# One pool of equal pages, and an encoder's first mixer interleaved in another order with its neighbours

## The chip, the core and the metric

The kernel runs on one NeuronCore of a Trainium2 chip, as one program. Five engines have instruction streams of their own: TensorE (PE in the profile; PEld is its weight load), VectorE (DVE), ScalarE (ACT), GpSimd (POOL) and SyncE (SP), of which SP and POOL mostly issue DMAs. An engine executes its stream in the order in which it was written; semaphores connect the streams. The metric is the device time of one execution in microseconds (us).

## The reference

A residual stream x of 1024 tokens by 1024 channels, fp32, goes through two layers. Each normalises x, shifts and scales it by a vector computed from the condition c (`ada_w`), applies a mixer, adds the gated result to x, and does the same with a SwiGLU feed-forward. Layer 0's mixer is the one that matters here:

```python
def attention_rwkv_mixer(h, cos, sin, w_in, w_out, ...):
    p = h @ w_in
    q, k, v = ...                      # 8 query heads, 2 key/value heads of 64
    q = apply_rope(rms_norm(q, q_norm), cos, sin)
    k = apply_rope(rms_norm(k, k_norm), cos, sin)
    y_attn = blocked_gqa(q, k, v)      # softmax(q k^T / 8) v, 512 channels
    y_rwkv = rwkv7_bidirectional(p[..., ATTN_IN:], ...)   # 512 channels
    return concat([y_attn, y_rwkv]) @ w_out
```

`rwkv7_bidirectional` runs a recurrence with a 64 by 64 state per head forward and backward over the tokens, adds both, normalises each head's 64 channels (`ln_g`, `ln_b`), adds a bonus and multiplies by a gate. Layer 1's mixer is a Hyena: a projection to three streams, short convolutions, and two long convolutions, whose filters come from a small network of the position and depend on no activation, then an output projection.

## The kernel before, in words

**Products.** Activations stand transposed, channels on the partitions, in tiles of 128 channels by 1024 tokens. Every large operand is split into a high and a low part in a shortened format: `split` lets ScalarE round the high part (L256) and VectorE subtract it (L257). A product is then three: high by high, high by low, low by high (`mm3`, L296), over two halves of 512 tokens. The feed-forward has its own form with seven products of blocks (L600 to L602).

**Pages.** SBUF is cut into equal pages of 128 partitions by 4 KB, handed out first in, first out: `page` takes the one longest free, `free` appends. There are two stacks, one for fp32 and one for the split operands; `repage` re-cuts the space between them between stages, and `fence`, `zone` and `low` keep certain pages from being handed out. An instruction that writes a page handed out anew waits for those that last used it; a DMA's wait stands on the engine that issues it, ahead of all that engine's later issues.

**Order.** Each part is a Python generator that emits a few instructions and yields. `weave` takes the generator that is furthest behind in proportion to its weight; `some(g, n)` takes n steps from g. So the order on every engine is fixed when the program is built.

**The first layer.** `norm_h` makes the normalised activations. The input projection (`stream`) runs over tiles of 128 output channels, with weights loaded on SP (L274), first RWKV tiles (their mixing steps with the neighbouring tokens are L1036, L1045 to L1047) with six attention tiles inserted, of which k and q are normalised and turned (L533, L541, L853). Beside it run `ada(1)` and the first steps of the first RWKV unit (`rwkv_x`, L1187, L1332). A unit is one direction of one pair of heads, eight in all. Then a loop weaves, per iteration i, `rwkv_s` (the scan of unit i-2; L1457 is a step's product, L1458 its state update, L1472 and L1475 its outputs) with a later part of unit i-1, the start of unit i, and n steps of `other`, which is attention (scores L924 and L925, softmax L928 to L932, transposes L947, values) followed by the sixteen Hyena filters (L1740, L1754, L1653, stored by POOL at L1764). After its second scan a pair of heads goes through `rwkv_post`: sums over each head (L1497), L1498, a square (L1501), sums (L533), the root and its inverse (L498, L501, L502), which are spread again (L541), then L1510, L1512, L1513. The result goes to DRAM (`sp_yr`), as do attention's (`sp_ya`).

**After the loop.** The attention half of the output projection (`project`, `matvec_add`, all tokens) and then the other half (`matvec_halves`, one token half after the other) load their operands, split them and add the gated product to x (L787), which the second half does as the feed-forward's normalisation asks for it.

**The Hyena.** Its split weights are loaded from DRAM in pieces (`hwi...` of the input projection, `hwo...` of the output projection) on POOL; L1630 is another operation of POOL's stream.

## Time and profile before

| | us |
|---|---|
| three runs | 3453.62, 3456.78, 3461.62; median 3456.78 |
| the profiled execution | 3456.75 |
| its span (first to last instruction) | 3454.8 |
| TensorE busy in the span | 3248.2 (94%) |
| VectorE busy | 2358.4 (68%) |
| ScalarE busy | 1252.9 (36%) |
| mean granted TensorE clock | 0.964 |

The last loop iteration of the mixer (the scan of the eighth unit) lies from 1238 to 1353 us, the projection behind it until about 1465, the feed-forward until 1900, the Hyena's mixer until 2750. In a row of a timeline stand the start, the duration, engine and line, the operation with its output and inputs, how often it comes in the group, and in brackets the idle time before it and what ended it. A row of DMA issues gives the time of the issue, not of the transfer.

### The profile page before, as it was taken

The numbers are of one execution on the slowest core, as the hardware profiler recorded it, in microseconds if no ns is written. First come the engines' busy times: TensorE is split into PE (matmuls) and PEld (weight loads), VectorE is DVE, ScalarE is ACT, GpSimd is POOL, SyncE is SP. The second block draws the span as 40 slices with busy tenths as digits, with TensorE's granted clock in tenths as the row PEclk, the third lists the DMA queues.
The fourth block names the chain that finished last, engine by engine and source line by source line (L and its number), as shares of the span: only waits on it lengthen the run. The fifth ranks groups of instructions, "written<-read, shape, count | busy, mean of one in ns | idle before, by whom it ended". The sixth has DMA issues, their size and how long they took to land.

```text
span 3454.8 us, 52847 instructions
## 1 busy us (share of the span) xinstructions
PE 3248.2 (94%) x20739; PEld 2635.1 (76%) x20739; DVE 2358.4 (68%) x4281; ACT 1252.9 (36%) x2296; POOL 245.0 (7%) x509
## 2 busy tenths in 40 slices
PE   8899889999999997999999999989977799999998
PEld 5687767777677896888888887777866688888887
DVE  5466465656667777597877667588997776667545
ACT  4632265555554442343233333221220243333211
POOL 2000000000011221000000220000000000000000
PEclk9999999999999998999999999999998899999999
DMA  7654522233332326244455993324335522224411
GB/s 260 226 174 147 162 62 72 59 87 80 82 104 71 94 81 201 80 128 146 134 162 191 356 359 129 119 80 140 128 127 206 173 78 93 74 73 137 142 50 49
DMA packets 332536, 459.29 MB, mean 133 GB/s; under 512 B 102968, under 2 KB 234897, under 8 KB 332288
## 3 DMA queue, kind: packets, MB, share of 16 engines
q1 hardware_dynamic: 292576, 322.04, 30.4%
q0 software_dynamic: 39536, 133.81, 11.3%
q8 instruction: 163, 2.67, 0.3%
q14 instruction: 85, 0.70, 0.1%
q10 hardware_dynamic: 176, 0.07, 0.0%
HBM read 311.66 MB, written 141.56 MB: 131 GB/s over the span
## 4 chain that ended last, share of the span: by engine, by line
PE 62%; DVE 8%; DMA 4%; issue 3%; ACT 2%; POOL 0%; DVEq 0%; SPq 0%; ACTq 0%; POOLq 0%
PE bk L296 21%; PE bk L601 8%; PE bk L602 8%; PE bk L600 8%; PE bk L1754 3%; DVE p L1653 2%; PE bk L1740 2%; PE bk L1775 2%; DMA p<-in_hy_w_in_dram 1%; PE bk L1928 1%; PE bk L947 1%; PE bk L1268 1%; PE bk L1332 1%; PE bk L1785 1%; PE bk L964 1%
## 5 line engine op out<-in xcount | busy, mean ns | idle before, releaser
L296 PE MATMUL bk<-p,p 128*128 128x512 f32 x5136 | 1242.8, 401 | 72.9 <-ACT p L256 33.2
L296 PEld LDWEIGHTS bk<-p,p 128*128 128x128 f32 x5136 | 980.7, 193 | 298.0 <-ACT p L256 36.0
L256 ACT ACTIVATE p<-p 128x512 fp32r<-128x512 f32 (+3 forms) x534 | 398.4, 761 | 950.8 <-PE bk L601 287.8
L257 DVE TENSOR_TENSOR p<-p,p 128x512 fp32r<-128x512 f32 (+3 forms) x534 | 445.7, 850 | 255.2 <-ACT p L256 215.6
L600 PE MATMUL bk<-p,p 128*128 128x512 f32 x1248 | 486.3, 391 | 2.7 <-ACT p L256 1.4
L601 PE MATMUL bk<-p,p 128*128 128x512 f32 x1248 | 486.0, 390 | 2.5 <-DVE p L257 2.5
L602 PE MATMUL bk<-p,p 128*128 128x512 f32 x1248 | 484.6, 390 | 0.0
L600 PEld LDWEIGHTS bk<-p,p 128*128 128x128 f32 x1248 | 234.5, 188 | 52.4 <-ACT p L256 4.3
L601 PEld LDWEIGHTS bk<-p,p 128*128 128x128 f32 x1248 | 235.0, 188 | 51.7 <-DVE p L257 3.3
L602 PEld LDWEIGHTS bk<-p,p 128*128 128x128 f32 x1248 | 234.6, 188 | 48.8
L787 DVE SCALAR_TENSOR_TENSOR p<-bk,mod,p 128x512 f32<-128x512 f32 x192 | 134.8, 744 | 90.0 <-PE bk L296 86.8
L1653 DVE TENSOR_TENSOR p<-p 128x128 f32<-128x128 f32 (+2 forms) x544 | 174.1, 384 | 0.2 <-ACT p L1309 0.2
L429 DVE SCALAR_TENSOR_TENSOR p<-p,cond,p 128x512 f32<-128x512 f32 x140 | 104.6, 748 | 54.3 <-DMA p<-in_ada_w_dram 52.1
L1754 PE MATMUL bk<-p,p 128*128 128x128 f32 x1024 | 135.0, 287 | 0.0
L1754 PEld LDWEIGHTS bk<-p,p 128*128 128x128 f32 x1024 | 125.9, 199 | 5.6 <-issue 2.0
L928 DVE TENSOR_REDUCE mx<-bk 128x1 f32<-128x512 f32 x128 | 87.1, 686 | 56.5 <-PE bk L925 55.4
L1742 ACT ACTIVATE p<-delta,k_tneg 128x128 f32<-128x128 f32 x256 | 86.9, 393 | 70.4 <-PE bk L1754 10.2
L1036 ACT COPY p<-bk 128x512 f32<-128x512 f32 (+1 forms) x80 | 43.9, 588 | 182.9 <-DVE p L1802 63.6
L948 ACT COPY p<-bk 128x512 f32<-128x512 f32 x128 | 74.1, 587 | 95.5 <-PE bk L947 94.2
L932 ACT ACTIVATE p<-bk,mx 128x512 f32<-128x512 f32 x128 | 86.9, 686 | 34.9 <-DVE mx L929 34.2
L947 PE MATMUL bk<-k_ident,p 128*128 128x128 f32 x512 | 85.0, 293 | 15.3 <-ACT p L932 14.8
L478 ACT ACTIVATE p<-p 128x512 f32<-128x512 f32 x80 | 49.9, 633 | 126.2 <-DVE p L814 117.6
(407 smaller groups left out, 4392.4 us busy)
## 6 DMA issues: line engine op xcount, KB each, us to landing
p<-in_ffn_w_dram SPq DMA_DIRECT2D x120, 512.0 KB, 4.8
p<-in_ada_w_dram SPq DMA_DIRECT2D x96, 512.0 KB, 4.4
sp_f<-p POOLq DMA_DIRECT2D x36, 512.0 KB, 5.5
p<-sp_f POOLq DMA_DIRECT2D x36, 512.0 KB, 5.7
hs<-p POOLq DMA_DIRECT2D x64, 256.0 KB, 3.2
p<-hs SPq DMA_DIRECT2D x32, 512.0 KB, 4.2
p<-sp_r SPq DMA_DIRECT2D x24, 512.0 KB, 4.8
p<-sp_x SPq DMA_DIRECT2D x24, 512.0 KB, 4.4
```

The source lines that it names most:

```text
L256: self.nc.scalar.activation(out=hi, in_=src, func=AF.Copy)
L257: self.nc.vector.tensor_tensor(out=lo, in0=src, in1=hi.bitcast(F32), op=ALU.subtract)
L296: nc.tensor.matmul(ps[n], a, b[:, HALVES[n]], start=s, stop=e)
L429: nc.vector.scalar_tensor_tensor(out=acc, in0=wt[:, i], scalar=self.cond[:, k : k + 1], in1=acc, op0=ALU.mult, op1=ALU.add)
L600: nc.tensor.matmul(ps, op[:, 0, k], mh, start=start and k == 0, stop=False)
L601: nc.tensor.matmul(ps, op[:, 0, k], ml, start=False, stop=False)
L602: nc.tensor.matmul(ps, op[:, 1, k], mh, start=False, stop=stop and k == 3)
L787: nc.vector.scalar_tensor_tensor(out=xs, in0=ps[n], scalar=self.modc(layer, part, m), in1=xs, op0=ALU.mult, op1=ALU.add)
L928: nc.vector.tensor_reduce(out=m[:, n : n + 1], in_=ps[n], axis=AX.X, op=ALU.max)
L947: nc.tensor.transpose(pt[:, j], pr[:, k * P : (k + 1) * P], self.ident)
L1653: tt = lambda o, a, b, op: nc.vector.tensor_tensor(out=o, in0=a, in1=b, op=op)
L1754: nc.tensor.matmul(ps[:, j, ri], F[2 * d + t2 // 4][:, t2 % 4, 128 * ri : 128 * ri + 128], tp[:, j, d], start=d == 0, stop=d == 1)
```

## The change

There is one pool of 46 pages, each of which may hold either kind of operand; `repage`, `fence`, `zone` and `low` are gone. Attention's six tiles in the projection move: k and the first two q from places 13, 15, 17 to 10, 11, 12, and v, last, from 21 to 20. `early` emits, beside the projection, the first RWKV unit's start and then the first step of attention (the keys, the first queries and the first scores). Attention loads its values only when it needs them. In the loop the steps of `other` change so that the filters end before the last iteration, and there `other` becomes `mix_out`: the attention half of the output projection, a fourth of a product at a time (`fine`), then the weights and the first three operands of the other half. The last pair of heads is split where it is made (`pair`), without the trip through DRAM. `project` gives x in SBUF (`kept`) to the second half.

```diff
-        self.stacks = {F32: [], F32R: []}
-        self.pages = {F32: deque(), F32R: deque()}
+        self.pages = deque()
...
+    def paging(self, ctx, n):
+        self.sb = ctx.enter_context(self.tc.tile_pool(name="sb", bufs=1))
+        self.pages.extend(range(n))
+        self.n = 0
...
-        t = next(z[dt] for z in self.zone if z[dt]).popleft()
+        i = self.pages.popleft()
+        self.n += 1
+        t = self.sb.tile([P, PAGE], dt, tag=f"pg{i}", name=f"p{self.n}")
+        self.page_of[t.tensor.name] = i
...
-                dt, t, _ = self.page_of[a.tensor.name]
-                assert all(t is not q for q in self.pages[dt])
-                self.put(t)
+                self.pages.append(self.page_of.pop(a.tensor.name))
...
+    def matvec_add(self, xT, w, ys, layer, part, g=0, keep=None, fine=False):
...
-                self.mm3(ps, [(wt[0][:, k, o : o + P], wt[1][:, k, o : o + P]) for k in range(nk)], ys)
+                wk = [(wt[0][:, k, o : o + P], wt[1][:, k, o : o + P]) for k in range(nk)]
+                for k in range(nk):
+                    self.mm3(ps, wk[k : k + 1], ys[k : k + 1], k == 0, k == nk - 1)
+                    if fine and k < nk - 1:
+                        yield
...
+            if "v" not in st:
+                st["v"] = self.page((P, 8, P))
+                nc.gpsimd.dma_start(out=st["v"].rearrange("p a b -> p (a b)"), in_=self.vd)
+            v = st["v"]
...
-                    self.fence(F32R, first=4)
...
-            out[hp] = self.rwkv_post(ys.pop(hp), hp, G)
+            out[hp] = self.rwkv_post(ys.pop(hp), hp, G, hp == 3)
...
+        if pair:
+            return self.split(y)
...
-        tiles = self.rwkv_tiles()
-        for i, t in zip((13, 15, 17, 19, 20, 21), self.attn_tiles()):
-            tiles.insert(i, t)
-        weave((250, self.stream(w, h, tiles)), (60, ada(1)), (30, first()))
-        for a in h:
-            self.free(a)
-        self.repage(42, 4)
-        self.set_banks(4, 4)
+        other = None
+
+        def early():
+
+            yield from first()
+            while not {"k", 0} <= set(self.qd):
+                yield "wait"
+            yield from some(other, 1)
...
+        tiles = self.rwkv_tiles()
+        for i, t in zip((10, 11, 12, 17, 19, 20), self.attn_tiles()):
+            tiles.insert(i, t)
+        weave((250, self.stream(w, h, tiles)), (60, ada(1)), (32, early()))
+        for a in h:
+            self.free(a)
+        self.set_banks(4, 4)
         for i in range(1, len(units) + 2):
             if i == len(units):
                 self.free(self.scanm)
-            n = (0, 48, 48, 48, 48, 50, 48, 46, 50, 48)[i]
+            n = (0, 48, 50, 52, 54, 54, 54, 62, 84, 36)[i]
+            if i > len(units):
+                run(other)
+                other = tail([out[x] for x in range(4)], outr)
...
-        for _ in other:
-            pass
+        run(other)
         self.set_banks(8)
-        return [out[i] for i in range(4)] + [outr[i] for i in range(4)]
...
+    K.paging(ctx, 46)
...
-    def project(xT, ys, w, layer, g=0):
+    def project(xT, ys, w, layer, g=0, **how):
 
         y = [K.split(K.unspill(d)) for d in ys]
         yield
-        yield from K.matvec_add(xT, w, y, layer, 2, g)
+        yield from K.matvec_add(xT, w, y, layer, 2, g, **how)
...
+    def mix_out(ya, yr):
+
+        w = ins["mix_w_out"][0]
+        yield from project(xd, ya, w[:512], 0, 1, keep=kept, fine=True)
+        y = []
+        steps.append(K.matvec_halves(kept, w[512:], y, 0, 2))
+        for i in range(3):
+            y.append(K.split(K.unspill(yr[i])))
+        while 3 not in yr:
+            yield
+        y.append(yr[3])
...
-    w = ins["mix_w_out"][0]
-    ys = K.mixer(ins["mix_w_in"][0], h, ada)
-    K.repage(13, 33)
-    xT = [K.unspill(d) for d in xd]
-    run(project(xT, ys[:4], w[:512], 0))
-    xT, steps = K.ffn(xT, halves(xT, ys[4:], w[512:], 0), 0, ada1(), hy_weights(), 20)
+    kept, steps = [], []
+    K.mixer(ins["mix_w_in"][0], h, ada, mix_out)
+    xT, steps = K.ffn(kept, steps[0], 0, ada1(), hy_weights())
```

The line numbers of the changed kernel differ: its L258 is the old L296, L883 and L884 are L924 and L925, L906 is L947, L1294 is L1332, L495 and L503 are L533 and L541, L1419 is L1457, L1434 and L1437 are L1472 and L1475, L1459 is L1497, L236 is L274 and L168 is L206. In the rows p is a page, bk a PSUM bank.

On TensorE, the end of the mixer's loop before, from the last sums of heads on:

```order
L1497 MATMUL bk_66<-p_158,k_blkones 128x512
L1754 MATMUL bk_68<-p_82,p_102 128x128
...
L1754 MATMUL bk_64<-p_3006,p_130 128x128
L1497 MATMUL bk_63<-p_158,k_blkones 128x512
L533 MATMUL bk_70<-k_blk_77,p_3010 128x2 x8
L541 MATMUL bk_65<-k_ident,rc_1277 64x128 x8
L541 MATMUL bk_63<-k_ident,rc_1277 64x128 x8
L296 MATMUL bk_66<-p_234,p_11458 128x512
```

All of the projection's products (L296) stand behind the last L541. And now, from the scan's last output on; p_12287 is the high part of the last pair of heads:

```order
L1459 MATMUL bk_64<-p_11372,k_blkones 128x512
L258 MATMUL bk_67<-p_12230,p_12211 128x512
L258 MATMUL bk_67<-p_12229,p_12212 128x512
...
L258 MATMUL bk_69<-p_12235,p_12218 128x512
L495 MATMUL bk_65<-k_blk_77,p_12254 128x2 x8
L258 MATMUL bk_65<-p_12223,p_12199 128x512
...
L258 MATMUL bk_65<-p_12235,p_12200 128x512
L503 MATMUL bk_66<-k_ident,rc_1151 64x128 x8
L503 MATMUL bk_70<-k_ident,rc_1151 64x128 x8
L258 MATMUL bk_66<-p_12223,p_12205 128x512
...
L258 MATMUL bk_70<-p_12235,p_12206 128x512
L258 MATMUL bk_64<-p_12287,p_12199 128x512
```

The filters' products between the sums have given way to products of the second half's first three operands, and 18 products now follow the last L503 ahead of the first that needs the last pair. Further ahead, the 192 products of the attention half stand between the scan's steps, but for the last five:

```order
L1434 MATMUL bk_66<-p_9435,p_10870 64x64
L1434 MATMUL bk_66<-p_9436,p_10870 64x64
L1437 MATMUL bk_66<-p_11525,p_11896 64x64 x2
L1434 MATMUL bk_66<-p_9435,p_10870 64x64
L1419 MATMUL bk_64<-p_11896,p_11524 64x64 x2
...
L258 MATMUL bk_67<-p_12223,p_12211 128x512
L258 MATMUL bk_67<-p_12224,p_12211 128x512
...
L258 MATMUL bk_69<-p_12229,p_12217 128x512
L1419 MATMUL bk_64<-p_11896,p_11524 64x64 x10
L1437 MATMUL bk_65<-p_11525,p_11896 64x64 x2
```

A step of the scan (two L1419) stood between filters before; the ten L1419 in one row are the last five steps.

On TensorE, attention's first scores before, behind the whole projection:

```order
L296 MATMUL bk_65<-p_554,p_258 128x512
L296 MATMUL bk_65<-p_550,p_482 128x512
L1332 MATMUL bk_70<-p_98,p_138 64x64 x11
L551 MATMUL bk_66<-k_ident,p_118 128x128 x3
L541 MATMUL bk_64<-k_ident,rc_2105 64x128 x8
L541 MATMUL bk_63<-k_ident,rc_2105 64x128 x8
L551 MATMUL bk_66<-k_ident,p_118 128x128
L1332 MATMUL bk_70<-p_98,p_138 64x64 x5
L551 MATMUL bk_64<-k_ident,p_118 128x128 x4
L1332 MATMUL bk_63<-p_98,p_142 64x64 x16
L924 MATMUL bk_64<-p_234,p_242 128x512
```

Here nothing of the projection (L296) is left to stand behind the first L924. And now, where the first scores stand in the last tiles' products and the first transposes (L906) behind the last of them:

```order
L495 MATMUL bk_63<-k_blk_77,p_2775 128x2 x7
L883 MATMUL bk_68<-p_2726,p_2734 128x512
...
L495 MATMUL bk_63<-k_blk_77,p_2775 128x2
L258 MATMUL bk_64<-p_414,p_2676 128x512
...
L884 MATMUL bk_68<-p_2727,p_2734 128x512
L884 MATMUL bk_69<-p_2727,p_2734 128x512
L258 MATMUL bk_65<-p_414,p_2677 128x512
...
L258 MATMUL bk_70<-p_419,p_2782 128x512
L1149 MATMUL bk_65<-p_2432,k_blkones 128x512
L883 MATMUL bk_68<-p_2726,p_2735 128x512
L884 MATMUL bk_68<-p_2727,p_2735 128x512
...
L906 MATMUL bk_69<-k_ident,p_2754 128x128 x4
```

L883 has moved ahead of the last tile's L258, and the first L906 behind them.

On SP, at the start of the kernel, the issues from the last constant of the first group to the first weight of the projection, before:

```order
L114 DMA k_eye_671<-in_k_eye_dram 128x64
L1526 DMA p_146<-in_k_scanm_dram 128x1040
L830 DMA p_150<-in_k_rope_c_dram 128x1024
L831 DMA p_154<-in_k_rope_s_dram 128x1024
L206 DMA sp_x_700<-p_94 128x1024
L206 DMA sp_x_714<-p_98 128x1024
L274 DMA p_158<-in_mix_w_in_dram 128x8x128
L206 DMA sp_x_740<-p_102 128x1024
```

The first weight (L274) stands behind two stores of x. And now, where eight stores of x and more small loads stand ahead of that weight:

```order
L108 DMA k_eye_460<-in_k_eye_dram 128x64
L1582 DMA hy_w<-in_hy_f_w_dram 33x64
L168 DMA sp_x_498<-p_125 128x1024
...
L168 DMA sp_x_847<-p_132 128x1024
L1584 DMA hy_w<-in_hy_f_w_dram 64x64 x2
...
L108 DMA k_tneg<-in_k_tneg_dram 128x16
L1030 DMA p_563<-in_rwkv_w_up_dram 64x2x512 x2
L1491 DMA p_468<-in_k_scanm_dram 128x1040
L791 DMA p_470<-in_k_rope_c_dram 128x1024
L792 DMA p_471<-in_k_rope_s_dram 128x1024
L236 DMA p_474<-in_mix_w_in_dram 128x8x128
```

The first weight (L236) has moved behind all of these, the weights of L1030 (before: L1067) among them.

More of the change, by code (lines that the diff above doesn't have):

```diff
@@ L553, in to_tok, with ffn @@
             self.fbank(pt)
-    def ffn(self, xT, before, layer, up=iter(()), down=iter(()), low=None):
+    def ffn(self, xT, before, layer, up=iter(()), down=iter(())):
         nc = self.nc
@@ L884, in attention @@
         nc = self.nc
-        v = self.page((P, 8, P))
-        nc.gpsimd.dma_start(out=v.rearrange("p a b -> p (a b)"), in_=self.vd)
         st = {}
@@ L996, in attention @@
                 yield from values(*steps[i - 1][:2])
-        self.free(st["k"], v)
+        self.free(st["k"], st["v"])
     def rwkv_spec(self):
@@ L1517, in rwkv_post, with mixer @@
         return d
-    def mixer(self, w, h, ada):
+    def mixer(self, w, h, ada, tail):
         self.rwkv_consts()
```

60 lines of the change are left out of this document (4 added, 56 removed).

## The prediction

> **What bounds the kernel now.** First the page's busy times. TensorE is busy for 94% of the span, VectorE for 68%:
>
> ```profile
> PE 3248.2 (94%) x20739; PEld 2635.1 (76%) x20739; DVE 2358.4 (68%) x4281; ACT 1252.9 (36%) x2296; POOL 245.0 (7%) x509
> ```
>
> The change leaves the products as they are, so the 3248.2 us of TensorE work stay. What can move is the 206.6 us of the span (3454.8 less 3248.2) in which TensorE stands idle, and the slower clock just after such gaps. A table of windows then finds the gaps: the mixer's loop by its iterations (the start, iterations 6 to 9), then the projection behind it.
>
> ```profile
> 427.00:514.00 87.00, 73.88 (x838) 55.54 (x840) 59.47 (x122) 52.56 (x122) 3.09 (x7) 0.90 0.25 64
> 917.00:1027.00 110.00, 100.96 (x1238) 81.14 (x1236) 72.58 (x196) 56.12 (x134) 14.27 (x25) 0.97 0.24 74
> 1027.00:1142.00 115.00, 103.57 (x1166) 89.86 (x1166) 82.64 (x237) 49.76 (x136) 21.24 (x34) 0.93 0.34 81
> 1142.00:1238.00 96.00, 96.00 (x1178) 85.33 (x1178) 64.73 (x198) 44.67 (x124) 22.91 (x35) 0.96 0.32 91
> 1238.00:1353.00 115.00, 90.58 (x733) 82.03 (x729) 94.01 (x278) 42.23 (x105) 27.78 (x42) 0.89 0.52 167
> 1365.00:1465.00 100.00, 100.00 (x459) 83.27 (x458) 51.23 (x78) 31.27 (x51) 0.00 (x0) 1.00 0.22 74
> ```
>
> After the stretch come PE, PEld, DVE, ACT and POOL busy, then the granted clock. Two rows stand out, with clocks of 0.90 and 0.89: the first loses 13.1 us, the last iteration 24.4 us. The last row gives the price of one long product with TensorE full: 100/459 = 0.218 us. The feed-forward stages are full in the same way and have nothing to give.
>
> **Part one, the mixer's end.** The timeline shows the 24.4 us as three gaps in one chain, the normalisation of the last head pair and its trip through DRAM:
>
> ```profile
> 1317.90 0.69 DVE L1498 SCALAR_TENSOR_TENSOR p<-bk,p 128x512 f32<-128x512 f32 x1 [0.36 <-PE bk L1497]
> 1324.38 1.04 ACT L1501 ACTIVATE p<-p 128x1024 f32<-128x1024 f32 x1
> 1325.48 2.57 PE L533 MATMUL bk<-k_blk,p 128*128 128x2 f32 x16 [3.18 <-ACT p L1501]
> 1329.21 1.28 ACT L501 ACT_TABLE_LOAD   x1
> 1334.33 3.68 PE L541 MATMUL bk<-k_ident,rc 128*64 128x128 f32 x32 [6.28 <-DVE rc L502]
> 1338.68 1.40 DVE L1510 SCALAR_TENSOR_TENSOR p<-p,cols,bk 128x512 f32<-128x512 f32 x2
> 1340.11 1.28 DVE L1512 SCALAR_TENSOR_TENSOR p<-p,cols,p 128x1024 f32<-128x1024 f32 x1
> 1343.33 1.22 DVE L1513 TENSOR_TENSOR p<-p,p 128x1024 f32<-128x1024 f32 x1
> 1345.96 0.32 SPq L211 DMA_DIRECT2D p<-sp_ya  x1
> 1351.86 1.06 ACT L256 ACTIVATE p<-p 128x1024 fp32r<-128x1024 f32 x1 [6.22 <-DMA p<-sp_ya]
> 1352.96 12.30 PE L296 MATMUL bk<-p,p 128*128 128x512 f32 x44 [14.96 <-ACT p L256]
> ```
>
> 3.18 + 6.28 + 14.96 = 24.42, the window's whole idle time. The slow clock adds 44 products in 12.30 instead of 9.6 us (2.7) and 32 L541 in 3.68 us against the 1.97 they take at 421.81 (1.7). Together 28.8 us.
>
> The new order puts 192 products of the attention half (192 x 0.218 = 41.9 us) and 54 of the other half (11.8 us) beside the scan, where before the filters stood. What is left bare, step by step: five scan steps without a product between them, each a wait for one L1458 and its handover (0.28 us and about 0.2, an estimate), 5 x 0.45 = 2.2; the handover to the first L1497, 1.1; L1498 and L1501 (1.73) lie under 17 products (3.7), 0; from L533 to L541 the table load 1.28 and three short steps, some 2.5, under 9 products (2.0), 0.5; from L541 the chain 1.40 + 1.28 + 1.22 + 1.06 = 4.96, with handovers 5.8, under 18 products (3.9), 1.9. That is 5.7. I add 2 for the clock after several short gaps (a gap of 1.3 us is followed by slow products in a row of part three), and 3 because VectorE, which runs in order, also has the residual adds and splits of the projection in this stretch.
>
> The moved step also brings its own loads: sp_ya, the weights and eight sp_x on SP's queue, where before they were issued during the filters' tail. The first products stand on TensorE ahead of the scan's next L1457, so if a load is late, the scan is too. The nearest row is the load above, 5.9 us from issue to L256. From 0 (loaded ahead) to 6; I take 4, since one page of it comes free only with the last filters' stores. After: 5.7 + 2 + 3 + 4 = 14.7. **Gain 14** (7 to 21).
>
> **The filters moved.** They no longer stand beside the last scan but in iterations 6, 7 and 8 (some 2, 1 and 2.7 filters more than before, by the order). Iterations 9 and 8 differ by 1.9 filters and 94.01 - 64.73 = 29.3 us of VectorE, so about 15 each. VectorE then has 72.58 + 29 = 102, 82.64 + 15 = 98 and 64.73 + 41 = 105 us. TensorE gets at least the 8.4 us of a filter's L1754, to 117, 112 and 118:
>
> ```profile
> L1754 PE MATMUL bk<-p,p 128*128 128x128 f32 x1024 | 135.0, 287 | 0.0
> ```
>
> 135.0/16 = 8.4. So TensorE stays the bound, by a narrower margin. **Cost 3** (-4 to +8): iterations 6 and 7 had 9.0 and 11.4 us of gaps, which more filter work may fill, or attention and scan may wait longer for the fuller VectorE.
>
> **Part two, the mixer's start.** Attention's first scores wait for the rope's normalisation and then their softmax stalls TensorE:
>
> ```profile
> 421.81 1.97 PE L541 MATMUL bk<-k_ident,rc 128*64 128x128 f32 x32
> 429.93 1.97 PE L1332 MATMUL bk<-p,p 64*64 64x64 f32 x32 [4.82 <-DVE p L853]
> 432.14 2.08 PE L924 MATMUL bk<-p,p 128*128 128x512 f32 x4 [0.24 <-ACT p L894]
> 434.02 1.88 PE L925 MATMUL bk<-p,p 128*128 128x512 f32 x4
> 443.77 1.97 PE L947 MATMUL bk<-k_ident,p 128*128 128x128 f32 x8 [7.88 <-ACT p L932]
> ```
>
> 4.82 + 0.24 + 7.88 = 12.9 idle, and the eight products take 3.96 instead of 8 x 0.218 = 1.7 us: 15.1. Now keys and the first queries are projected earlier and L924 and L925 stand among the last tile's products, with 55 of them (12.0 us) between the first pair of L925 and the first L947. From the end of L925 to L947 it was 7.9 us, so this gap goes. What is late next is the last projected tile, now a value tile of the RWKV half. Its mixing steps are:
>
> ```profile
> 83.54 1.15 ACT L1046 ACTIVATE p<-p,mu 128x1024 f32<-128x1024 f32 x1
> 84.50 1.23 DVE L1045 TENSOR_TENSOR p<-p 128x1024 f32<-128x1024 f32 x1
> 85.83 1.28 DVE L1047 SCALAR_TENSOR_TENSOR p<-p,mu,p 128x1024 f32<-128x1024 f32 x1
> ```
>
> About 3.7 us with copies and handovers 5, under scores, transposes and L1332 of similar length. I leave 4 us idle and 2 for slow clock. **Gain 9** (3 to 14).
>
> **Part three, one pool.** At the start of the kernel the order of SP's issues changes. Before:
>
> ```profile
> 36.37 0.33 SPq L114 DMA_DIRECT2D k_eye<-in_k_eye_dram  x1
> ...
> 41.95 0.95 SPq L274 DMA_DIRECT2D p<-in_mix_w_in_dram  x1
> ...
> 53.92 1.22 PE L296 MATMUL bk<-p,p 128*128 128x512 f32 x2
> ...
> 58.23 1.02 SPq L274 DMA_DIRECT2D p<-in_mix_w_in_dram  x2
> ...
> 69.92 15.74 PE L296 MATMUL bk<-p,p 128*128 128x512 f32 x61 [1.10 <-DVE p L257]
> ...
> 91.42 1.22 PE L1085 MATMUL bk<-p,p 128*128 128x512 f32 x2 [5.76 <-DVE p L1071]
> ```
>
> From k_eye to the second weight there were 18 issues in 21.9 us, 1.2 each. Now the first weight has 20 issues between k_eye and itself, so it is issued at about 36.4 + 24 = 60.4, 18 us later, and its products begin near 68 instead of 53.9 (issue, transfer and split, about 8 us, less than the first one's 12 since the queues are emptier). But then 96 run in one piece, 20.9 us, to 89, where before they were broken up and L1085 came at 91.42, because its weights were issued at 76.95; now those go ahead. **0** (-5 to +9).
>
> Behind the first feed-forward, the hyena's projection waits for loads issued by POOL, which itself stands behind a wait for VectorE:
>
> ```profile
> 2136.18 8.61 PE L296 MATMUL bk<-p,p 128*128 128x512 f32 x24 [1.30 <-DMA p<-hwi1l]
> 2164.16 8.57 PE L296 MATMUL bk<-p,p 128*128 128x512 f32 x25 [4.83 <-DMA p<-hwi8h]
> POOL p L1630 <- DVE p L522: 18.9, 1, 18.9
> ```
>
> Idle 6.1, slow clock 3.4 + 3.1, together 12.6. In the new order the load behind the second gap waits on products some 70 places ahead of its use (15 us), the load behind the first on some 25 (5.5 us, about the length of a load). **Gain 5** (-4 to 12).
>
> One rule of the Trainium skill is weighed here. The first of these rows is slow, 8.61 us for 24 products, after a gap of 1.30 only. The page "TensorE: Matmul & The Clock Gate" (section "HAM oscillation — how this bites in real kernels") has the clock fall only where TensorE idles for more than some 3.4 us at a time. By it the short gaps left at the mixer's end would cost no clock, part one would gain 16, and the sum below would be 2 us lower. The row disagrees with it, so the 2 us stay.
>
> Inside the hyena VectorE is the limit, and loads wait for pages:
>
> ```profile
> 2550.00:2600.00 50.00, 37.64 (x194) 31.60 (x192) 50.00 (x86) 13.14 (x19) 4.54 (x11) 0.90 0.66 229
> 2665.52 8.52 PE L296 MATMUL bk<-p,p 128*128 128x512 f32 x24 [2.93 <-DVE p L787]
> 2683.23 5.62 PE L296 MATMUL bk<-p,p 128*128 128x512 f32 x12 [9.18 <-DMA p<-hwo11h]
> 2693.41 3.78 PE L1951 MATMUL bk<-p,p 128*128 128x128 f32 x16 [4.56 <-DVE p L1653]
> ```
>
> One queue of pages gives each load the page longest free, which shortens some waits; but pages last read by VectorE now also serve weights. From a gain of 20 (2.93 + 9.18 + 4.56 and the slow 3.3) to a loss of 12, one more wait like hwo11h's (9.18 and 3.0 of slow clock). Nothing here says which; I take **0**.
>
> **The sum.** The profiled execution took 3456.75 us, 1.95 around its span, and the median of the three runs is 3456.78, the same. 3456.75 - 14 + 3 - 9 + 0 - 5 + 0 = 3431.75, so **3432 us**, 0.7% faster.
>
> **Rivals.** *A, the last scan's new neighbours cost what they save.* TensorE takes its queue in order; if the attention half's operands come late, scan and products both wait, and the filters crowd VectorE. For it: VectorE goes above 80% in iterations 6 to 8. Against it: the loads are issued ahead of the scan. With part one at 0 and the filters at +7: 3456.75 + 7 - 9 - 5 = 3450.
>
> *B, slower: weights wait for VectorE's pages in the hyena.* Before, weight pages and working pages were apart; now a weight's load on POOL may stand behind a VectorE operation, and every load behind it on POOL. Each costs 12 us by the row at 2683.23. Two cost what the forecast gains; with three, 3432 + 36 = 3468. For it: VectorE's 50.00 of 50. Against it: 46 pages serve all, and loads stand further ahead.
>
> *C, the hyena's waits go too.* The 20 us above are taken away: 3412. For it: hwo11h waited for a page, not for the transfer. Against it: VectorE's work there is unchanged.
>
> **Chances and range.** Forecast 0.55, A 0.15, B 0.17, C 0.13. No change means within 0.2%, 7 us, which is what a measurement can tell: faster is the forecast but for 0.03, C and a third of A, 0.70; same 0.13; slower, B, 0.17. The forecast's own range is 3417 to 3447; with A, C and the near part of B 3410 to 3462.
>
> **What would show it.** Right: in the last iteration attention-half products between scan steps, no gap over 4 us before the feed-forward; the first L947 without a gap of 7 us; L296 at some 68 us in one row of 96; no wait for hwi8h. Wrong: an L1457 or L296 waiting on sp_ya for over 6 us; VectorE above 90% in iterations 6 to 8 with gaps on TensorE; new waits for hwo or hwi loads.

## The result and the profile after

The changed kernel takes 3487.43 us (median of 4 runs, 3483.32 to 3490.62) against 3455.2 before: the ratio is 1.0081, with an interval of 1.0059 to 1.0104. It is slower, where 0.7% faster was forecast, and it lies outside the range. The forecast's side was wrong.

The profiled execution took 3490.62 us. The first row of its page already shows what the prediction had ruled out (PE, PEld, DVE, ACT, POOL busy):

```profile
PE 3276.4 (94%) x20739; PEld 2627.6 (75%) x20739; DVE 2362.7 (68%) x4281; ACT 1249.8 (36%) x2294; POOL 243.4 (7%) x509
```

The number of products is the same, 20739, but TensorE is busy for 3276.4 instead of 3248.2 us. Idle time is 212.0 us where it was 206.6. To see where the 28 us sit, one takes a stretch in which TensorE never waits and nothing was changed: the second feed-forward, the same 300 us in both kernels. Before:

```profile
2850.00:3150.00 300.00, 300.00 (x1325) 248.51 (x1324) 203.54 (x318) 97.17 (x158) 7.45 (x14) 1.00 0.23 80
```

After:

```profile
2850.00:3150.00 300.00, 300.00 (x1298) 243.39 (x1298) 202.39 (x311) 95.21 (x153) 8.52 (x16) 1.00 0.27 84
```

Both are busy throughout at the full granted clock, but one gets through 1325 products and the other through 1298: 0.2264 against 0.2311 us each, 2.1% more. This is so in every stage. The kernel has 8880 such products (5136 of the projections, 3744 of the feed-forwards); 8880 x 0.0047 = 42 us, an estimate that takes each of them to stand on the path. Each single gain that the prediction worked out is smaller than this one row.

The places that the prediction did look at went much as it said. At the start, the first weight is issued late and its 96 products run in one piece:

```profile
55.03 5.82 SPq L236 DMA_DIRECT2D p<-in_mix_w_in_dram  x3
```

```profile
65.78 24.43 PE L258 MATMUL bk<-p,p 128*128 128x512 f32 x96 [8.82 <-ACT p L218]
90.05 0.62 PE L1048 MATMUL bk<-p,p 128*128 128x512 f32 x2
```

They begin at 65.78 (forecast 68) and end at 90, where L1048 follows at once; before, the same line (L1085) came at 91.42. At the mixer's start the scores stand among the projection's products and the gap of 7.88 us ahead of the first transposes is gone:

```profile
410.54 0.63 PE L884 MATMUL bk<-p,p 128*128 128x512 f32 x2
...
428.87 1.04 PE L906 MATMUL bk<-k_ident,p 128*128 128x128 f32 x8
...
435.04 2.48 PE L1294 MATMUL bk<-p,p 64*64 64x64 f32 x42 [2.84 <-DVE p L1150]
```

And at the mixer's end the chain of three gaps (24.4 us) has come down to a few short ones:

```profile
1308.34 0.34 PE L1434 MATMUL bk<-p,p 128*64 128x64 f32 x4 [1.16 <-DVE p L1406]
1309.48 6.76 PE L258 MATMUL bk<-p,p 128*128 128x512 f32 x28 [0.80 <-DVE p L219]
1320.63 2.08 PE L258 MATMUL bk<-p,p 128*128 128x512 f32 x4 [4.39 <-ACT p L218]
...
1371.21 0.33 PE L1419 MATMUL bk<-p,p 64*64 64x64 f32 x4
1371.93 0.33 PE L1419 MATMUL bk<-p,p 64*64 64x64 f32 x4 [0.39 <-DVE p L1420]
...
1374.96 0.48 PE L1437 MATMUL bk<-p,p 64*64 64x64 f32 x4 [0.39 <-DVE p L1420]
...
1396.38 2.63 PE L503 MATMUL bk<-k_ident,rc 128*64 128x128 f32 x32
1398.99 25.64 PE L258 MATMUL bk<-p,p 128*128 128x512 f32 x108
```

The late load costs 4.39 us (forecast 4), the bare scan steps five times 0.39 (forecast 2.2 in all), and behind the last L503 nothing waits (forecast 1.9). The feed-forward then begins at 1435.3 instead of 1444.1 us. But the iterations ahead of it have become long, and they hold more: 1324, 1301 and 1403 products, where the prediction's table has 1238, 1166 and 1178. These are the windows of iterations 6 to 8, and of iteration 9 with the projection in it:

```profile
917.10:1044.30 127.20, 117.32 (x1324) 100.90 (x1323) 83.98 (x244) 59.49 (x152) 23.27 (x37) 0.96 0.37 100
1044.30:1178.80 134.50, 120.14 (x1301) 105.29 (x1298) 101.80 (x309) 56.42 (x160) 29.71 (x47) 0.95 0.39 101
1178.80:1305.80 127.00, 126.48 (x1403) 112.27 (x1402) 95.51 (x281) 57.15 (x156) 29.45 (x45) 1.00 0.34 104
1305.80:1435.30 129.50, 118.93 (x630) 90.13 (x628) 68.63 (x121) 30.15 (x43) 2.99 (x4) 0.92 0.38 129
```

From there to the feed-forward it was 527 us before and is 518 now. But from the first scan (its first VectorE operation) to 917 us it was 403 us (from 514.3) and is 415 (from 502.1). The loop starts 12 us earlier, is 12 us longer up to 917 us and 9 shorter from there on: over the whole loop 930 us have become 933. In the hyena, POOL's loads now wait for VectorE. Its waits in that stage before:

```profile
POOL p L271 <- PE bk L296: 240.3, 15, 68.6
```

and after (L233 is the same loading line):

```profile
POOL p L233 <- DVE p L1799: 60.3, 2, 30.9
POOL p L233 <- DVE p L1775: 50.0, 1, 50.0
...
POOL p L233 <- DVE p L1784: 37.9, 5, 10.5
```

### The profile page after: what moved, and what is told of

Its sections match the earlier page's. It is cut to its first block, busy times and chain, and to the rows that moved or that the text cites. A ratio compares the mean times of both kernels' runs of the same rounds, so it can differ in the third digit from the quotient of the medians.

```text
span 3488.4 us, 52479 instructions
## 1 busy us (share of the span) xinstructions
PE 3276.4 (94%) x20739; PEld 2627.6 (75%) x20739; DVE 2362.7 (68%) x4281; ACT 1249.8 (36%) x2294; POOL 243.4 (7%) x509
## 5 line engine op out<-in xcount | busy, mean ns | idle before, releaser
L258 PE MATMUL bk<-p,p 128*128 128x512 f32 x5136 | 1255.7, 403 | 86.1 <-ACT p L218 43.6
L258 PEld LDWEIGHTS bk<-p,p 128*128 128x128 f32 x5136 | 975.4, 192 | 324.3 <-ACT p L218 46.2
L218 ACT ACTIVATE p<-p 128x512 fp32r<-128x512 f32 (+2 forms) x534 | 396.0, 760 | 929.4 <-PE bk L564 248.8
L219 DVE TENSOR_TENSOR p<-p,p 128x512 fp32r<-128x512 f32 (+2 forms) x534 | 444.3, 850 | 205.7 <-ACT p L218 169.7
L1728 PE MATMUL bk<-p,p 128*128 128x128 f32 x1024 | 134.5, 286 | 3.3 <-DVE p L1717 3.3
L1728 PEld LDWEIGHTS bk<-p,p 128*128 128x128 f32 x1024 | 124.6, 198 | 9.4 <-DVE p L1717 3.9
L1677 ACT COPY p<-bk 128x256 f32<-128x256 f32 (+1 forms) x80 | 33.0, 413 | 202.7 <-PE bk L1728 106.6
L1294 PE MATMUL bk<-p,p 64*64 64x64 f32 x2048 | 88.3, 226 | 15.1 <-DMA p<-o 9.6
L1294 PEld LDWEIGHTS bk<-p,p 64*64 64x64 f32 x2048 | 74.5, 138 | 34.4 <-issue 12.5
```

Of the source, the lines that this page charges most:

```text
L218: self.nc.scalar.activation(out=hi, in_=src, func=AF.Copy)
L219: self.nc.vector.tensor_tensor(out=lo, in0=src, in1=hi.bitcast(F32), op=ALU.subtract)
L258: nc.tensor.matmul(ps[n], a, b[:, HALVES[n]], start=s, stop=e)
L1294: nc.tensor.matmul(pt[H[p], pr], lhs(e, pr, p), rhs[H[p], 8 * e + pr], start=True, stop=True)
L1728: nc.tensor.matmul(ps[:, j, ri], F[2 * d + t2 // 4][:, t2 % 4, 128 * ri : 128 * ri + 128], tp[:, j, d], start=d == 0, stop=d == 1)
```

## The experiments

Ratios are to the kernel before as it ran in the same set, with their intervals. Time is the median. The kernel before itself came out between 3448 and 3457 us from one set to the next, so runs of different sets are better compared by their ratios.

| run | us | ratio |
|---|---|---|
| changed kernel again | 3484.96 | 1.0100 (1.0085 to 1.0115) |
| before, wide pages | 3481.59 | 1.0079 (1.0054 to 1.0103) |
| changed, pages of 1056 | 3476.44 | 1.0074 (1.0051 to 1.0098) |
| changed, pages of 1088 | 3453.55 | 1.0008 (0.9994 to 1.0021) |
| changed, gaps between pages | 3457.27 | 1.0013 (0.9996 to 1.0030) |
| ... no tail | 3427.03 | 0.9926 (0.9903 to 0.9949) |
| ... no early scores | 3451.27 | 1.0002 (0.9985 to 1.0019) |
| ... pool only | 3435.47 | 0.9954 (0.9937 to 0.9972) |
| ... both beside the scan | 3417.84 | 0.9908 (0.9880 to 0.9937) |
| ... no tail, pages apart | 3417.19 | 0.9890 (0.9862 to 0.9919) |
| ... table whole, pages apart | 3443.76 | 0.9962 (0.9947 to 0.9977) |
| ... both beside, pages apart | 3411.74 | 0.9882 (0.9861 to 0.9903) |
| ... the same, table's early part | 3422.95 | 0.9927 (0.9904 to 0.9950) |
| ... the same, table's late part | 3419.85 | 0.9917 (0.9894 to 0.9940) |
| ... the same, no early scores | 3414.58 | 0.9887 (0.9853 to 0.9921) |

Rows with "..." have pages of 1088 numbers.

### Does the pace of the products belong to the kernel?

The first two runs are the two kernels unchanged.

> The kernel before, unchanged, profiled on the chip of this job. In the two profiles so far a 512-wide product L296 starts 226.8 us/1000 after the one ahead of it in the kernel before and 231.4 in the changed one, in every stage. If the chip makes that difference, this profile shows 231 ns too. If the kernel makes it, 227 ns and about 3455 us.

> The changed kernel, unchanged. If the pace of the products belongs to the kernel: again 231 ns and about 3487 us. If it belonged to the chip of the first profile: possibly 227 ns, and then 8880 products x 4.6 ns = 41 us less, about 3446 us.

The kernel before took 3446.8 us in its one run, with 0.2267 us from one wide product's start to the next in the second feed-forward, the changed one 3484.96 and 0.2314. On one and the same chip each keeps its pace, so it is the kernel's own.

### The width of a page

The pages of the kernel before were not all equal, as the description ahead has it: those of fp32 were 1040 numbers wide (4160 bytes), those of split operands 1024 (4096). What the change does everywhere, in all stages alike, is to put the split operands into pages of 1040 numbers too. This can be done to the kernel before, without any of the rest:

```diff
-                u = self.tc.tile([P, PAGE if dt == F32 else 1024], dt, name=name, side=side)
+                u = self.tc.tile([P, PAGE], dt, name=name, side=side)
```

> The kernel before with the pages of the split operands 1040 numbers wide (4160 bytes) instead of 1024 (4096), as the one pool has them; order unchanged. Theory pages: the products' operands no longer lie at multiples of 4096 bytes from each other, so products take 231 ns, and the time is about 3455 + 41 = 3496 us. Theory order or chip: 227 ns, 3455 us.

And the changed kernel can be given other pages:

```diff
-        t = self.sb.tile([P, PAGE], dt, tag=f"pg{i}", name=f"p{self.n}")
+        t = self.sb.tile([P, 1088], dt, tag=f"pg{i}", name=f"p{self.n}")
```

> The changed kernel with all 46 pages 1088 numbers wide (4352 bytes, a multiple of 256) instead of 1040. Theory pages, if a distance that is a multiple of 256 bytes is enough: 227 ns, about 3446 us. If it must be 4096, or the pages do nothing: 231 ns, 3487 us.

Both came out on the side that the theory of the pages has, and at 31 us where it set 41: 31 us slower than the kernel before by that one line (3481.59 against 3450.26; 27 by the ratio), and 31 us faster than the changed kernel by the other (3453.55 against 3484.96). TensorE's busy time in the profile rose by 35.4 us with the wide pages, to 3283.6. The windows of the second feed-forward say the same, first the kernel before with wide pages, then the changed kernel with pages of 1088:

```profile
2850.00:3150.00 300.00, 300.00 (x1298) 243.40 (x1297) 199.76 (x313) 95.17 (x155) 8.53 (x16) 1.00 0.25 85
```

```profile
2850.00:3150.00 300.00, 300.00 (x1326) 248.47 (x1325) 206.64 (x317) 97.77 (x157) 7.47 (x14) 1.00 0.24 78
```

1298 and 1326 products: the pace has gone over with the page. Two more runs ask what of the page it is. One leaves the rows 1040 wide and puts 48 unused numbers behind each:

```diff
+        for i in range(n):
+            self.sb.tile([P, PAGE], F32, tag=f"pg{i}", name=f"q{i}")
+            self.sb.tile([P, 48], F32, tag=f"gap{i}", name=f"gap{i}")
```

> The changed kernel with its pages 1040 numbers wide, but with 48 unused numbers behind each, so that they lie 4352 bytes apart as in after_1088. If the distance of the pages in SBUF sets the pace of the products: 0.2267 us each and about 3454 us, like after_1088. If it is the row width in the products' access patterns (1040 against 1088): 0.2314 us each and 3485 us, like after_again.

The other makes the page 1056 numbers wide, 4224 bytes, by the same line as above.

> The changed kernel with pages of 1056 numbers, 4224 bytes, a multiple of 128 but not of 256. If a multiple of 128 is enough: 0.2267 us a product, about 3454 us. If it takes 256: between 0.2267 and 0.2314, 3465 to 3487 us.

With gaps:

```profile
2850.00:3150.00 300.00, 300.00 (x1325) 248.40 (x1324) 204.82 (x314) 97.37 (x157) 7.46 (x14) 1.00 0.25 83
```

With pages of 1056:

```profile
2850.00:3150.00 300.00, 300.00 (x1302) 244.20 (x1301) 204.40 (x314) 96.64 (x156) 8.53 (x16) 1.00 0.25 81
```

So it is the distance of the pages in SBUF, not the width written in the access pattern. Distances of 4096 and 4352 bytes, multiples of 256, are fast; 4160 and 4224 are slow. A multiple of 128 is not enough. Nor need a page begin at a multiple of 256: in the program of the kernel before all operands of wide products lie 224 bytes past one, with pages of 1088 all lie 160 past.

A product's own two addresses do not tell its pace: grouped by them, the products of the slow kernels differ by some 2 ns at most. But the products around it do. In the kernel with pages of 1056 an operand lies at 32 or at 160 bytes past a multiple of 256. Joining each product of the trace with its addresses in the program, and counting for how many products running both operands of all of them had had one and the same remainder, gives this (start to next start):

```
products in a row with one remainder    1      2      3      4      5      6      7      8     over 8
mean ns                               230.5  231.9  230.0  230.1  229.2  228.8  229.0  227.6  227.4
number of them                         2099   1037    247    209    133    120     61     34    90
```

After some eight products of one remainder the pace is within 1 ns of that of the kernel before. It is the same if only products are counted that stand thirteenth or later in an unbroken row of wide ones. The kernel with pages of 1088 has such an approach only where a row begins, from 233 ns at the second product to 226.8 from the eleventh on; the one with 1056 stays at 231 all along the row. The grouping is not an experiment, and what in the reading of the operands makes it so stays open. That equal remainders modulo 256 for all pages are enough is shown, for distances of 4096 and 4352 bytes.

### Part one without the page width

After the pages are mended the changed kernel is no faster than before (1.0008). Where did the 25 us of the forecast go? The next runs undo one part each. The first undoes the mixer's end: table of steps, filters beside the last scan, projection behind the loop, last pair through DRAM.

```diff
-            n = (0, 48, 50, 52, 54, 54, 54, 62, 84, 36)[i]
-            if i > len(units):
-                run(other)
-                other = tail([out[x] for x in range(4)], outr)
+            n = (0, 48, 48, 48, 48, 50, 48, 46, 50, 48)[i]
...
-            out[hp] = self.rwkv_post(ys.pop(hp), hp, G, hp == 3)
+            out[hp] = self.rwkv_post(ys.pop(hp), hp, G, False)
...
+    xT = [K.unspill(d) for d in xd]
+    run(project(xT, ys[:4], w[:512], 0))
```

> after_1088 with the mixer's end as before: the loop's table of steps, the filters beside the last scan, the whole output projection behind the loop, the last pair through DRAM. By the prediction's part one and its cost of the moved filters (14 gained, 3 lost) this is 11 us slower than after_1088 (3453.55): 3464 us. Rival: before's time varies by some 10 us at this very place between executions, and the moved filters cost what the end gains: 3454 us, no difference.

It is not 11 us slower but 27 faster, 3427.03 against 3453.55. Both expectations fell. So part one, which closes the gaps as forecast, costs more than it gives. It has two halves, though: a table of steps that clears the last iteration of filters, and the projection that takes their place. The next kernel keeps the projection, the direct split of the last pair, and the filters too:

```diff
-            n = (0, 48, 50, 52, 54, 54, 54, 62, 84, 36)[i]
+            n = (0, 48, 48, 48, 48, 50, 48, 46, 50, 90)[i]
...
-                run(other)
-                other = tail([out[x] for x in range(4)], outr)
+                other = chain(other, tail([out[x] for x in range(4)], outr))
```

> after_1088 with the loop's old table, so that filters stay beside the last scan, and the attention half of the projection behind them in the same iteration (90 steps in all), the last pair still split where it is made. If the moved filters cost the 26 us that no_tail gained: about 3427 us, or some 4 us less as the end's last waits go. If the projection's products beside the scan cost them: still about 3450 us.

3417.84: the loss is in the table, not in the projection's products beside the scan. Against no_tail the projection's new place is worth 9 us at the medians, though the intervals overlap; with pages apart (below) it is 0.9882 against 0.9890, nothing. What the table does in the loop is seen best in two kernels that differ in it and in what it leaves beside the last scan, table_apart and both_apart. This is the whole loop, from the first scan to the feed-forward, with the changed table:

```profile
496.30:1429.60 933.30, 879.86 (x9338) 699.62 (x9334) 608.43 (x1533) 443.38 (x1057) 99.98 (x161) 0.96 0.34 92
```

and with the old one:

```profile
499.60:1402.30 902.70, 861.39 (x9338) 692.16 (x9335) 608.92 (x1535) 445.84 (x1060) 100.02 (x161) 0.97 0.34 94
```

The same 9338 products, 30.6 us longer: 12.1 us more idle time (53.4 against 41.3) and 18.5 us more in the products themselves. VectorE's work is the same and is at 65%, so it is not the bound over the loop.

The idle time comes in short waits: 36 of 0.15 to 1 us, together 17.3 us, against 15 with 6.9, while the longer ones make 34 us in either loop. And most of the 18.5 us is the clock. Rounded to 0.96 and 0.97 it looks almost the same, but in the traces it stands at half speed for 78.5 us of the first loop and 58.0 us of the second, and 435 and 268 of the products start in these stretches. By what products of the same lines take at full clock they cost some 30 and 18 us more than that, an estimate from the two traces: 12 of the 18.5 us. The last iteration shows it, first with the changed table, then with the old one; look at the clock, ahead of the last two numbers:

```profile
1302.10:1429.60 127.50, 116.97 (x630) 89.55 (x628) 68.60 (x121) 30.11 (x43) 2.99 (x4) 0.93 0.38 132
1214.70:1402.30 187.60, 180.57 (x1135) 154.70 (x1135) 140.41 (x341) 64.52 (x139) 27.73 (x41) 0.99 0.42 143
```

The other 6.5 us are products that are dearer at full clock, above all the wide ones (238.8 ns against 231.6) and the filters' first ones (306 against 294), and why they are stays open. The halves of the table were then taken singly.

```diff
-            n = (0, 48, 48, 48, 48, 50, 48, 46, 50, 90)[i]
+            n = (0, 48, 50, 52, 54, 54, 48, 46, 50, 74)[i]
```

> both_apart (3411.74 us) with the changed table's numbers for iterations 2 to 5 only (attention ahead by 16 steps), so that 16 filter steps leave the last iteration. If attention set forward is what the table costs: most of the 36 us between after_1088 and both_beside come back, some 3440 us. If the filters in iterations 6 to 8 are: near 3412.

```diff
-            n = (0, 48, 48, 48, 48, 50, 48, 46, 50, 90)[i]
+            n = (0, 48, 48, 48, 48, 50, 54, 62, 84, 34)[i]
```

> both_apart with the changed table's numbers for iterations 6 to 8 only (54, 62, 84), so that 56 filter steps leave the last iteration and attention stays where it was. If the filters moved into iterations 6 to 8 are what the table costs: some 3440 us. If attention set forward is: near 3412.

The whole table, with filters cleared from the last iteration, is the changed order with pages of 1088 divided in the hyena:

> The changed order whole (its table of steps, and no filter beside the last scan), pages 4352 bytes apart and divided in the hyena: both_apart with both halves of the table. If the halves add (early_table 11 and late_table 8 over both_apart's 3411.74): about 3431 us. If it is more than their sum, because the last scan then has no filter beside it at all: about 3445 us, as after_1088 less the hyena's few us.

By their ratios (0.9882 without): 0.9927 for the early half, 0.9917 for the late one, 0.9962 for the whole. So 15.5, 12 and 28 us, each uncertain by some 8 or more. Neither half alone holds the cost, so neither of the first two expectations was right. (The early half sets attention forward and with it takes 16 of the 72 filter steps out of the last iteration, the late half the other 56.) Whether the halves add up is not settled. By the ratios they do. By the plain times they make 11 and 8 us and the whole 32, and in the profiles the loop takes 902.7 us with neither, 909.8 and 909.6 with one, 933.3 with both. The third expectation set 3431 us for halves that add, and 3445 if a last scan without filters beside it costs something of its own; 3443.76 was measured. The 36 us between the medians of after_1088 and both_beside are more than 28, within what the intervals of both allow.

### Part two

```diff
-        for i, t in zip((10, 11, 12, 17, 19, 20), self.attn_tiles()):
+        for i, t in zip((13, 15, 17, 19, 20, 21), self.attn_tiles()):
...
-        weave((250, self.stream(w, h, tiles)), (60, ada(1)), (32, early()))
+        weave((250, self.stream(w, h, tiles)), (60, ada(1)), (30, first()))
```

> after_1088 with attention's tiles at their old places and no scores in the projection. By the prediction's part two: 9 us slower than after_1088, 3462 us, with the gap of 8 us before the first L947 back. Rival: the gap only moves, since scores, scan and attention share the engines: 3454 us.

> no_tail with attention's tiles and first scores at their old places too: of the change only the one pool is left, with pages 4352 bytes apart. If early scores are worth nothing without the tail either, as no_early showed with it: like no_tail, 3427 us. If the prediction's 9 us come out once the tail is gone: 3436 us. If the pool alone gives nothing: 3453 us.

> both_apart with attention's tiles and first scores at their old places. pool_only was 8 us over no_tail, no_early no different from after_1088. If early scores are worth the 9 us of the prediction once the loop is in its old order: 3420 us. If nothing: 3412 us.

With the whole change around it, the early scores are worth nothing (1.0002 without, 1.0008 with); in the best order nothing either (0.9887 and 0.9882); with the old end of the loop 0.9954 without and 0.9926 with, intervals that overlap. The gap ahead of the first L947 did go, as the row at 428.87 shows. In the profiles pool_only is 9 us behind no_tail at the first scan (507.5 against 498.5) and 3 at the feed-forward (1412.5 against 1409.5): the loop makes good what the start loses. Most of the gap only moved, as the rival had it.

pool_only is also the price of the pool by itself, once its pages lie right: 0.9954, 16 us faster than two stacks. Nearly all of it comes from the mixer's loop. From the first scan to the feed-forward, first the kernel before (before_again), then pool_only:

```profile
511.00:1438.00 927.00, 866.46 (x9327) 698.59 (x9324) 608.76 (x1533) 449.64 (x1059) 99.79 (x162) 0.95 0.34 92
507.50:1412.50 905.00, 862.13 (x9327) 693.39 (x9324) 605.65 (x1530) 442.60 (x1054) 99.85 (x161) 0.96 0.34 94
```

That is 22 us less, 17.7 of them idle time of TensorE. Behind the loop the pool loses 9 us, about half of it in the first feed-forward (439.1 us before, 443.5 now).

### Pages in the hyena

The prediction's rival B said that in one pool a weight's load waits for VectorE. This run gives the hyena two lists of pages again, out of the one pool, and returns to one list behind it:

```diff
-        i = self.pages.popleft()
+        i = (self.lists[dt] if self.lists else self.pages).popleft()
...
+    K.apart(20)
     ys = K.hyena(hw_in, h, lambda y: project(xd, y, hw_out[0], 1))
+    K.together()
```

> no_tail with the pages divided during the hyena's mixer, 20 for split operands and 26 for the rest, each page going back to its own list. If pages shared between weights and VectorE's tiles are what hold up the hyena (rival B of the prediction): TensorE's idle time between its first and last L1951 falls from 70 towards 58 us and the time by up to 10 us, to 3417 us. If VectorE's work bounds it: 3427 us.

> both_beside with the pages divided during the hyena's mixer as in no_tail_apart. no_tail_apart was 10 us under no_tail and both_beside 9 us under it. If the two gains add: about 3408 us, 1.2% under the kernel before. If no_tail_apart's 10 us came from elsewhere than the hyena (in its profile the hyena's stretch gained only 2 us), no more than both_beside: 3418 us.

Three pairs differ in this alone: 0.9926 to 0.9890, 0.9908 to 0.9882, 1.0008 to 0.9962, which is 12, 9 and 16 us; only the third pair's intervals lie apart. POOL's waits show that the loads no longer wait for VectorE, but for one. These are table_apart's in the hyena, with its loading line L252 and product lines L277, L1778 and L1944:

```profile
POOL p L252 <- PE bk L277: 118.7, 14, 25.6
POOL p L252 <- PE bk L1778: 75.1, 2, 69.8
POOL p L252 <- PE bk L1944: 54.9, 2, 54.1
...
POOL p L252 <- DVE p L1646: 10.7, 1, 10.7
```

Loads wait for products again, and once for a VectorE operation. But the place of the gain was not the one expected. In the profiles of no_tail and no_tail_apart TensorE's idle time between the first and the last product of the long convolutions (L1951 in the kernel before) fell only from 70.4 to 67.4 us, where the kernel before has 56.8, and the stretch is no shorter (387.4 and 388.6 us). What was gained stands ahead of it (3.0 us, of which 1.7 ahead of the division of the pages), between it and the second feed-forward (3.4) and in that (3.0). So the division gains time, and it takes the waits away; that the waits cost the time is not shown.

both_apart is the fastest of all, 3411.74 us, 1.2% under the kernel before and 2.0% under the changed one.

## Why the prediction was wrong

**The failed step is its first sentence on the change**, "The change leaves the products as they are, so the 3248.2 us of TensorE work stay." The products were the same in number, and not in price. The pool's pages are 64 bytes longer than the pages of split operands were, and that costs some 31 us of the final 32. The diff shows it in one line, `self.sb.tile([P, PAGE], dt, ...)`, where before stood `PAGE if dt == F32 else 1024`. The prediction read the line for which pages are shared and not for where they lie, and the profile of before could not show it, because all its split operands lay right. A smaller slip is in the price itself: 0.218 us for a long product is 100 us over 459 products, of which over 30 are narrow ones; alone, the wide ones take 0.2264.

**"The filters moved. Cost 3 (-4 to +8)"** is the second step that failed, and the largest error within what was argued: 28 us for the table. The step asked whether VectorE would become the bound, worked out 98 to 105 us of it in iterations 6 to 8, and took the loop as TensorE's. VectorE came out at 84, 102 and 95 us in the windows above, so that check held and did not help. Of the 30.6 us by which the two loops differ, 12 are idle time and some 12 more the half-speed clock, for which this step had no term.

**Part one's own chain was right in its waits.** Late load 4 (4.39), bare steps 2.2 (1.95), handover to L1497 1.1 (the first L1459 starts without a gap), the rest 2.4 (0.3, ahead of the 9 products behind L495). TensorE's idle time from the last unit's scan to the feed-forward fell from 24.4 to 10.6 us. As a change by itself it is worth 0 to 9 us, not 14: no_tail and pool_only, which have the pool and the old end, have only 9.6 and 11.2 us of idle time there, so the pool alone had taken most of the 24.4 away.

**Part two: 9 forecast, the gap closed, 0 to 10 measured.** The step that failed is that a gap closed at the loop's start is time saved at its end; the loop made good most of it either way.

**The start of the kernel, 0**, came out (1.4 us gained), in part by luck. The first weight was issued at 55.03, not 60.4: an issue took 0.9 us and not 1.2. From issue to first product it was 10.8 us, not 8, and the 96 products took 24.4 us, not 20.9. The errors nearly cancel. **The first feed-forward to the hyena, gain 5**: the waits for hwi8h and hwi1l are gone, one of 1.1 us for hwi1h has come, and idle time there fell from 9.9 to 4.8; the stage is no shorter (289.8 to 289.3 us), since its products had become dearer, and with mended pages it gains nothing either (286.6 in before_again, 288.3 in after_1088). **The hyena, 0 (-20 to +12)**: dividing the pages there gives 9 to 16 us, on rival B's side. Rival B's waits were there, but most of the gain lies outside the stretch of the long convolutions, where they were looked for. **One pool** was priced at the kernel's start and behind the first feed-forward alone. What it gives by itself, 16 us, comes from the mixer's loop, for which the sum has no such term.

**The rivals.** B had the right side, and its waits came, with a third of its 36 us to be had by removing them; its 3468 would still have been too low. Of A, that the last scan's neighbours come late cost 4 us, and that the filters cost more than forecast was right, at 28 us and not 7. C did not happen. No rival held the page's distance, or a loop that slows by its clock as much as by waits.

**The clock.** The prediction kept 2 us for slow clock after short gaps. The rows at 1371.93 to 1374.96 bear the mechanism out: at 1373.88, behind three gaps of 0.39 us and with none longer in the 50 us ahead, the granted clock falls to half, and groups of four small products take 0.48 us instead of 0.33. It stays there until 1384.12:

```profile
1376.00:1384.00 8.00, 8.00 (x57) 5.24 (x56) 2.55 (x4) 1.06 (x1) 0.00 (x0) 0.50 0.18 65
```

It falls once more, from 1394.36 to 1397.77. The size was too small: by what the same products take at full clock, the two stretches cost some 6 us, an estimate. The last window's clock of 0.92 has a third stretch in it, behind the gap of 4.39 us. The rule that the prediction weighed is that of the Trainium skill's page "TensorE: Matmul & The Clock Gate" (section "HAM oscillation — how this bites in real kernels"), by which idle gaps of more than about 3.4 us lower the clock. The fall at 1373.88 came without one.

## What to carry to other kernels

When an edit changes how buffers are laid out, look up where every operand of the main products now lies before pricing anything else: here pages 64 bytes longer, which no row of the profile shows, cost 31 us, more than the whole gain of 25 that was forecast. Compare the count of products in a stretch that is full in both kernels; it separates a dearer product from an idle engine in two rows. Do not take a mean clock of 0.96 and one of 0.97 as equal over a long stretch: over some 900 us they were 20 us more at half speed. And a gap that closes is a gain only when the stage behind it starts earlier: undo the part and see, since work that is moved into a full loop can cost more there than it saves where it was.

## What the runs showed of the hardware

- The pace of products with a 512-wide fp32r operand depends on the distance of the operands' pages: 0.2264 us at distances of 4096 and 4352 bytes, 0.2311 at 4160 and 0.2304 at 4224, throughout the program. The filters' fp32 products, 128 wide, did not change (L1754, later L1728, starts every 111 to 112 ns before and after).
- The effect is not of a single product's addresses (230.5 to 231.7 ns by them with pages of 1056). It fades over some eight products whose operands agree modulo 256 bytes (227.6 ns), by a grouping of one trace.
- The same 9338 products of the mixer's loop took 861.4 us of busy time in one weaving and 879.9 in another. The clock was at half speed for 58.0 and 78.5 us of it, which by an estimate makes 12 of the 18.5 us.
- The granted clock fell to half behind three gaps of 0.39 us, between groups of four small products (at 1373.88 in the changed kernel).
